# Deferring the first softmax map's normalisation to the merge, and putting each head's query and key projections next to each other

## The chip, the cores and the metric

The kernel runs on one core of a Trainium2 chip. The metric is the device time of one execution in microseconds, as the median of several executions. Before the change it is 1486.3 us (median of three, 1482.65 to 1487.47).

The core has five engines that run their own instruction lists in order and wait for each other through semaphores: PE (TensorE, matmuls, with its weight loads shown as PEld), DVE (VectorE), ACT (ScalarE), POOL (GpSimd) and SP (SyncE, which here only issues DMAs). PSUM holds what PE writes; SBUF holds everything else on chip.

## The reference

One layer of a streaming encoder works on 1024 new frames of a prompt and 32 frames of a running stream (together T = 1056 columns), with a model width of 1024. One wide input projection feeds two parallel branches, a gated linear attention (GLA, four heads) and a differential attention (eight heads); a merge joins them. In short, for the differential branch:

```python
s = einsum('bqhmd,bkhmd->bhmqk', q, k) * DIFF_HD ** -0.5     # m = 0, 1: two maps per head
p = softmax(where(mask, s, -inf), axis=-1)
attn = p[:, :, 0] - lam * p[:, :, 1]
o_diff = einsum('bhqk,bkhe->bqhe', attn, v)
yd = rmsnorm(o_diff, diff_subln_g) * (1 - lambda_init) * silu(dg)
merged = sigmoid(ma) * (yg @ w_proj_gla) + sigmoid(mb) * (yd @ w_proj_diff)
y = x + rmsnorm(merged @ w_out, post_norm_g)
```

`rmsnorm` divides by sqrt(mean square + EPS) over the 128 values of a head. The queries and keys are rotated (RoPE) over the first 16 of each map's 64 dimensions. The rotated keys and the values are outputs too.

## The kernel before

Every float32 matmul is done as three matmuls on a rounded high part and a remainder (`wh`, `wl` for weights; slots 0 and 1 of `X` for the input), so a 128-row block of a projection is 8 k-steps x 3 matmuls x 3 chunks of 352 columns.

The work has four stages. First the input is normalised and the value projections run (to about 240 us of the profiled execution). Then come the GLA heads (to about 557 us), the differential heads (to about 1180 us), and the merge: GLA output projection (`pg_first`, `pg_job`), differential output projection (`proj` with `BLK_PD`), and the output projection `wout`.

**The order on PE.** In the GLA and differential stages the order of PE's instructions is written out by a small planner, the class `Order` (`S`). Threads are generators; each `yield` gives a step's assumed cost, the events it needs with an assumed latency (table `W`), and the PSUM banks it takes. `S.run` always picks the first thread in its list that is ready in its own clock: the attention thread `diff_main`, then `sample_thread`, then `fill`. The plan is made when the program is built; on the chip PE follows the list in order and waits wherever an operand is late. The other engines' lists are laid out by the framework, with a higher priority for some copies.

**Jobs.** `fill` works through a list of projection jobs. For each chunk it takes one of two PSUM banks `pj`, issues 24 matmuls (L465 to L467) and calls the job's `evac`, which copies the bank; the planner has the bank back 1.5 us later (`w_pj`). A job's weights are loaded and split (L431 to L435) one job ahead. There are four sorts in the differential stage:

- `rot_job` for a query block (`split_q`) or key block (`split_k`): `evac` copies each chunk into the tile `rr` (L806, ACT). After the third chunk `done` copies four strips of `rr` into `sw` by DMA (L798, L799), multiplies `sw` on POOL (L800), does the rotation on DVE (L802, L804) and then splits `r` into high and low parts on ACT and DVE (L814 to L821 for the query, L833 to L841 for the key, the latter with a store of the key and four DMAs that copy the parts to the other half of the partitions). The tile `rr` has one buffer, so the next `rot_job`'s first copy follows the last reader of the one before. The query's parts have two buffers by head, the key's one.
- `dgate_job`: the silu gate of a head (L477, L478).
- `gate_job`: one block of the merge's sigmoid gates (L484), stored to memory at its end; the tile has one buffer.

The order of the jobs is the list built at L1037 to L1048: for each head the next head's query, one merge gate, the next head's key, this head's silu gate, and further merge gates where `GATES_DIFF` has more than one.

**Attention.** For each head and each block of 128 queries, `diff_scores` computes both maps' scores for w = 128 x (i + 1) keys (L883, L884), masks a corner (L885), takes the row maximum (L887), and exponentiates with the row sum accumulated (L889). Then one reciprocal of both sums (L892), one multiply of the second map (L893) and one multiply-add (L894) give the difference of the normalised maps. `diff_main` transposes it (L931), splits it (L933, L934) and multiplies by the values (L944 to L946). `diff_fin` takes the mean square of a head's output (`ps_m`, L859), stores it as a row of `msd`, multiplies the output by the silu gate and stores it to `ydd`.

**The merge's norm.** At L1130 to L1134 the eight rows of mean squares are loaded, turned into 1/sqrt(mean + EPS) by a logarithm and an exponential on ACT, stored to `rsd`, and read back broadcast over partitions (`rsb`, L1140); L1141 multiplies each head's `ydr` with it, then it is split into `Y` (L1069, L1070) for the differential output projection (L443 to L445).

Of the kernel before, what the change touches and what calls it, by code (L numbers as in the profile page):

```python
# [11 lines left out]
F32 = mybir.dt.float32  # L12
F32R = mybir.dt.float32r
I32 = mybir.dt.int32
AF = mybir.ActivationFunctionType
ALU = mybir.AluOpType
# [4 lines left out]
P = 128  # L21
NP = 1024
# [6 lines left out]
DH, HD = 8, 64  # L29
NQ = NP // P  # L30
EPS = 1e-6
# [20 lines left out]
W = {  # L52
# [3 lines left out]
    "tr_t": 2.27, "dv": 5.65, "at": 2.45, "pv_o": 1.1, "sdg": 1.84, "sdk": 21.35, "kc": 7.45, "ss_s": 3.69,  # L56
    "sp": 7.1, "st_t": 1.14, "sv": 3.44, "spt": 0.43, "so_o": 3.58, "so": 4.1, "so_t": 0.72, "yg0": 4.48,
    "yg": 1.18, "pg_b": 1.72, "sm": 1.98, "sm_w": 0.00141, "sm_s": 2.25, "p": 2.4, "p_w": 0.00204,
}


# [61 lines left out]
def hybrid_step_kernel(ctx: ExitStack, tc: tile.TileContext, a):  # L123
    nc = tc.nc
    mm = nc.tensor.matmul
    act = nc.scalar.activation
    ve = nc.vector
    dma = nc.sync.dma_start
    st = nc.sync.dma_start
# [4 lines left out]
    dram = ctx.enter_context(tc.tile_pool(name="dram", bufs=1, space=DRAM))  # L134
    cst = ctx.enter_context(tc.tile_pool(name="cst", bufs=1))
# [9 lines left out]
    def tbank(name):  # L145
        return pp.tile([P, 512], F32, tag="t", name=name)
# [5 lines left out]
    ident = cst.tile([P, P], F32, name="ident")  # L152
    make_identity(nc, ident)
    eps = cst.tile([P, 1], F32, name="eps")
# [23 lines left out]
    ptd = dram.tile([KT, P, T], F32, name="ptd")  # L178

    msd = dram.tile([DH, NP], F32, name="msd")  # L180
    rsd = dram.tile([DH, NP], F32, name="rsd")


# [7 lines left out]
    v1 = pool("v1")  # L191
# [138 lines left out]
    with tc.manual_schedule(engines={E.PE, E.Activation, E.DVE, E.Pool}):  # L330

        def warm(n):
            ps = obank("ps_warm")
            for _ in range(n):
                mm(ps[:, 0:P], one_h, one_h, start=True, stop=True)
        warm(10)
        norm_square(0)
        s = norm_scale(0)
        warm(9)
        w0 = value_weights(0)  # L340

        def weights(n):
            for _ in range(n):
                wv = next(w0)
            return wv
        weights(2)
        norm_apply(*s, 0)
        weights(1)
        norm_low(*s, 0)
        weights(2)  # L350
        norm_apply(*s, 1)
        norm_low(*s, 1)
        weights(3)
        norm_square(1)
        wv = weights(3)
        ps = bank("ps_v")

        def first(p, ks):
            for k in ks:
                mm(ps, xs[k][:, p == 1, 0:P], wv[p == 2][:, k, :], start=(p == k == 0), stop=(p == 2 and k == KT - 1))  # L360
        first(0, range(6))
        first(1, range(6))
        s = norm_scale(1)
        norm_apply(*s, 0)
        weights(1)
        norm_apply(*s, 1)
        for p, ks in ((0, (6, 7)), (1, (6, 7)), (2, range(8))):
            first(p, ks)
        norm_low(*s, 0)
        norm_low(*s, 1)  # L370
        norm_square(2)
        w0 = value_weights(1)
        nxt = weights(1)
        for i in range(1, NQ + 1):
            value_tile(0, i - 1, ps)
            if i == NQ:
                xsm = sample_pair(xs, "xsm")

            def meanwhile():
                norm_tile(i + 1)  # L380
                if i < NQ - 1:
                    norm_square(i + 2)
                if i in (3, 4, 5, 6):
                    weights(3 if i < 6 else 2)
            ps = value_mm(i, *wv, meanwhile)
        value_tile(0, NQ, ps)
        wgs = gate_weights()

        gg_half = cst.tile([P, 2], F32, name="gg_half")
        ve.tensor_scalar(gg_half, g_gla, 0.5, None, op0=ALU.mult)  # L390
        gs_half = cst.tile([P, 1], F32, name="gs_half")
        ve.tensor_scalar(gs_half, g_sub, 0.5 * (1.0 - LAM_INIT), None, op0=ALU.mult)


        lv = cst.tile([P, 4, HD], F32, name="lv")
        dma(lv, a["lamv"].unsqueeze(0).to_broadcast([P, 4, HD]))
        lp = cst.tile([P, 2, HD], F32, name="lp")
        ve.tensor_tensor(lp, lv[:, 0:2, :], lv[:, 2:4, :], op=ALU.mult)
        ls = cst.tile([P, 2], F32, name="ls")
        ve.tensor_reduce(ls, lp, axis=AX.X, op=ALU.add)  # L400
        le = cst.tile([P, 2], F32, name="le")
        act(le, ls, AF.Exp)
        neglam = cst.tile([P, 1], F32, name="neglam")
        ve.tensor_tensor(neglam, le[:, 1:2], le[:, 0:1], op=ALU.subtract)
        ve.tensor_scalar(neglam, neglam, LAM_INIT, None, op0=ALU.subtract)
        coef = cst.tile([P, 1], F32, name="coef")
        ve.memset(coef, 1.0)
        for r in (32, 96):
            ve.tensor_copy(coef[r : r + 32], neglam[r : r + 32])
        wv = nxt  # L410
# [9 lines left out]
    tp = pool("tp", side="right", reuse_waits="tile")  # L420


    S = Order({"pj": 2, "s": 2, "t": 1, "o": 1})
# [57 lines left out]
    def gate_job(b, w, j):  # L481
        def begin():
            th = rp.tile([P, T], F32, tag="gate", name="gate")
            return (lambda ps, sl: act(th[:, sl], ps, AF.Tanh, scale=0.5)), (lambda: st(thd[w, j], th))  # L484
        return b, ("gate", w, j), begin, []
# [242 lines left out]
    gates = [(BLK_MB + j, 1, j) for j in range(KT)] + [(BLK_MA + j, 0, j) for j in range(KT)]  # L728
# [18 lines left out]
    jobs = []  # L747
# [33 lines left out]
    def sam(n, h):  # L781
        return smp[:, 20 + 4 * n + h % 4, :]

    dqs, dks, dsg = {}, {}, {}

    def parts(n, cnt):
# [82 lines left out]
    def diff_scores(h, i, out):  # L869
        w = (i + 1) * P  # L870
        qsl = slice(i * P, i * P + P)
        qs, (ks, kls) = dqs[h], dks[h]
        sm = dp.tile([P, 2], F32, tag="sm", bufs=2, name="sm")
        pt = []
        soft = W["sm"] + w * W["sm_w"]
        for m in range(2):
            cost = sum(max(0.11, min(512, w - n0) / 2200) for n0 in range(0, w, 512)) * 2
            yield cost, [(("dk", h), W["dk"]), (("dq", h), W["dq"])], ["s"]
            ps = dbank("ps_s")

            for n0 in range(0, w, 512):
                n = min(512, w - n0)
                mm(ps[:, n0 : n0 + n], qs[m][:, qsl], ks[m][:, n0 : n0 + n], start=True, stop=False)  # L883
                mm(ps[:, n0 : n0 + n], qs[m][:, qsl], kls[m][:, n0 : n0 + n], start=False, stop=True)  # L884
            ve.memset(ps[0:64, w - 64 : w], -1e30)  # L885
            nm = dp.tile([P, 1], F32, tag=f"nm{m}", bufs=2, name="nm")
            ve.tensor_reduce(nm, ps[:, 0:w], axis=AX.X, op=ALU.max, negate=True)  # L887
            p = dp.tile([P, NP], F32, tag=f"p{m}", bufs=2 - m, name="p")
            act(p[:, 0:w], ps[:, 0:w], AF.Exp, bias=nm, accum_out=sm[:, m : m + 1])  # L889
            S.free("s", soft + W["sm_s"])  # L890
            pt.append(p)
        ve.reciprocal(sm, sm)  # L892
        ve.tensor_scalar(pt[1][:, 0:w], pt[1][:, 0:w], sm[:, 1:2], neglam, op0=ALU.mult, op1=ALU.mult)  # L893
        ve.scalar_tensor_tensor(pt[0][:, 0:w], pt[0][:, 0:w], sm[:, 0:1], pt[1][:, 0:w], op0=ALU.mult, op1=ALU.add)  # L894
        S.mark(("p", h, i))
        if i == NQ - 1:
            S.mark(("qk", h))
        out[i] = pt[0], soft + W["p"] + w * W["p_w"]

    def diff_main():  # L900
        fin = None
        for h in range(DH):
# [47 lines left out]
                S.mark(("pv", h, g))  # L950
            fin = diff_fin(h, osb, sqo)
        yield from fin

    def sample_thread():
        w = PAST + NS
# [82 lines left out]
    for h in range(-1, DH):  # L1038
        need = [(("qk", h - 1), 0.0)] if h >= 1 else []
        n = GATES_DIFF[h + 1]  # L1040
        if h + 1 < DH:
            jobs.append(rot_job(BLK_DQ + h + 1, ("dq", h + 1), need, split_q(h + 1)))
        jobs += [gate_job(*gates.pop(0)) for _ in range(min(n, 1))]
        if h + 1 < DH:
            jobs.append(rot_job(BLK_DK + h + 1, ("dk", h + 1), need, split_k(h + 1)))
        if h >= 0:
            jobs.append(dgate_job(h))
        jobs += [gate_job(*gates.pop(0)) for _ in range(n - 1)]  # L1048
    with tc.manual_schedule(engines=PE):
        left = S.run(left + [[diff_main(), None, first], [sample_thread(), None, nullcontext],  # L1050
                             [fill(jobs, xs), None, nullcontext]],
# [75 lines left out]
    Y = x_pair("Y")  # L1127
    yd = [Y[k // 6][:, k % 6] for k in range(KT)]

    rs = cp.tile([DH, NP], F32, tag="cwh", name="rs")  # L1130
    dma(rs, msd)
    act(rs, rs, AF.Ln, bias=eps[0:DH])
    act(rs, rs, AF.Exp, scale=-0.5)
    st(rsd, rs)  # L1134
    rsb = {}
# [165 lines left out]
```

## Time and profile before

| What | Value |
|---|---|
| Median of three runs | 1486.3 us (1482.65 to 1487.47) |
| The profiled execution's own time | 1483.59 us |
| Its span, first to last instruction | 1481.9 us |
| Mean granted TensorE clock | 0.99 |
| PE busy | 1422.6 us, 96% of the span |
| DVE busy | 786.6 us, 53% |
| ACT busy | 601.0 us, 41% |
| POOL busy | 298.4 us, 20% |

How to read the rows. A row of a stretch has the stretch, its length, then for PE, PEld, DVE, ACT and POOL the busy microseconds with the number of instructions, then the granted TensorE clock (1.00 is full speed), the DMA engines' busy share and the GB/s that they moved. A row of a group has the line, engine and operation, what is written from what, shapes and count; behind the bar the busy microseconds in all, the mean nanoseconds of one, and the idle time of the engine just before them with what ended it. A row of a timeline has start and duration in microseconds, engine, line and operation; the bracket is the idle time of the engine before it and what ended that. A wait for several semaphores is put down to one of them, so the name in a bracket can be another than the true one. PE's matmuls are pipelined and their durations overlap.

### The profile page before, as it was taken

Reading aid. Unit: us, or ns where it says so; the run is one execution under the profiler, and the core shown is the slowest. Engines: PE = TensorE matmul, PEld = TensorE weight load, DVE = VectorE, ACT = ScalarE, POOL = GpSimd, SP = SyncE. Lnnn points to the kernel's source line nnn. Section 1 sums busy time; section 2 is a strip of 40 time slices with the busy share of each in tenths; the row PEclk is TensorE's granted clock in tenths of the full one; section 3 lists DMA queues with packets and bytes.
Section 4 is the critical chain, followed back from the end, with each engine's and each line's share of the span. In section 5 each row is a group of like instructions: output and inputs, shape, how many; then the busy total and the mean of one; then the engine's idle time right before and its main releaser. Section 6 shows DMA issues by size and latency. Waiting matters only on the chain.

```text
span 1481.9 us, 22365 instructions
## 1 busy us (share of the span) xinstructions
PE 1422.6 (96%) x8848; PEld 1327.6 (90%) x8848; DVE 786.6 (53%) x1464; ACT 601.0 (41%) x1262; POOL 298.4 (20%) x186
## 2 busy tenths in 40 slices
PE   8999999989999999899999999999899899999997
PEld 6787789889989899899989998998899799999997
DVE  5702005755565343576767767678665535455415
ACT  5612114535344232455555555555455432221311
POOL 1200002222213224123222222222221111122001
PEclk9999999999999999999999999999999999999999
DMA  8621111122222233323232333223322278633205
GB/s 310 205 105 38 45 45 48 56 74 68 81 70 73 70 120 108 90 62 106 72 108 60 106 86 96 69 83 90 92 68 81 97 264 302 223 131 129 103 1 192
DMA packets 66742, 156.58 MB, mean 106 GB/s; under 512 B 10008, under 2 KB 28568, under 8 KB 65600
## 3 DMA queue, kind: packets, MB, share of 16 engines
q1 hardware_dynamic: 66624, 155.01, 32.3%
q8 instruction: 74, 1.21, 0.3%
q14 instruction: 44, 0.36, 0.1%
HBM read 104.39 MB, written 40.04 MB: 97 GB/s over the span
## 4 chain that ended last, share of the span: by engine, by line
PE 51%; DVE 6%; DMA 4%; ACT 2%; issue 1%; POOL 1%; SPq 0%; DVEq 0%; POOLq 0%; ACTq 0%
PE ps_w L465 9%; PE ps_w L466 9%; PE ps_w L467 9%; PE ps_w L444 2%; PE ps_w L443 2%; PE ps_w L445 2%; PE ps_s L884 2%; PE ps_t L931 2%; PE ps_s L883 2%; DMA ydr<-ydd 2%; PE ps_c L1193 2%; PE ps_c L1195 2%; PE ps_c L1194 2%; PE po L945 1%; PE po L946 1%
## 5 line engine op out<-in xcount | busy, mean ns | idle before, releaser
L465 PE MATMUL ps_w<-X,wh 128*128 128x352 f32 x1344 | 453.8, 338 | 8.5 <-DVE sg L478 3.2
L466 PE MATMUL ps_w<-X,wl 128*128 128x352 f32 x1344 | 438.2, 326 | 0.0
L467 PE MATMUL ps_w<-X,wh 128*128 128x352 f32 x1344 | 436.4, 325 | 0.0
L435 POOL TENSOR_TENSOR wl<-wr,wh 128x1024 fp32r<-128x1024 f32 x72 | 179.5, 2493 | 661.8 <-ACT wh L433 528.6
L465 PEld LDWEIGHTS ps_w<-X,wh 128*128 128x128 f32 x1344 | 255.8, 190 | 13.6 <-issue 4.9
L466 PEld LDWEIGHTS ps_w<-X,wl 128*128 128x128 f32 x1344 | 256.1, 191 | 1.2 <-issue 1.2
L467 PEld LDWEIGHTS ps_w<-X,wh 128*128 128x128 f32 x1344 | 255.1, 190 | 0.0
L889 ACT ACTIVATE p<-ps_s,nm 128x256 f32<-128x256 f32 (+7 forms) x128 | 94.6, 741 | 59.1 <-DVE ps_s L885 31.1
L286 PE MATMUL ps_v<-wh,X 128*128 128x512 f32 x248 | 97.6, 393 | 0.6 <-DVE X L225 0.6
L287 PE MATMUL ps_v<-wl,X 128*128 128x512 f32 x248 | 98.0, 395 | 0.0
L433 ACT ACTIVATE wh<-wr 128x1024 fp32r<-128x1024 f32 x72 | 75.9, 1054 | 54.6 <-PE ps_w L467 30.4
L285 PE MATMUL ps_v<-wh,X 128*128 128x512 f32 x248 | 97.9, 395 | 0.0
L887 DVE TENSOR_REDUCE nm<-ps_s 128x1 f32<-128x256 f32 (+7 forms) x128 | 94.8, 747 | 2.7
L272 DVE TENSOR_TENSOR vo<-ps_v,vo 32x512 f32<-32x512 f32 x4 | 2.7, 679 | 139.9 <-ACT vo L271 139.9
L885 DVE MEMSET ps_s<- 64x64 f32 x128 | 14.3, 112 | 115.8 <-PE ps_s L884 114.2
L650 POOL TENSOR_TENSOR vl<-vr,vh 128x512 fp32r<-128x512 f32 (+1 forms) x20 | 24.8, 1242 | 222.8 <-DVE t L516 160.3
L883 PE MATMUL ps_s<-k,q 128*128 128x512 f32 (+2 forms) x192 | 68.0, 362 | 1.2 <-DMA k<-k 1.2
L884 PE MATMUL ps_s<-kl,q 128*128 128x512 f32 (+2 forms) x192 | 63.8, 348 | 3.9 <-DMA kl<-kl 3.4
L268 ACT ACTIVATE vo<-ps_v 128x512 f32<-128x512 f32 x32 | 19.1, 596 | 114.2 <-PE ps_v L287 113.8
L933 ACT ACTIVATE ah<-ps_t 128x512 fp32r<-128x512 f32 (+2 forms) x96 | 46.9, 488 | 43.6 <-PE ps_t L931 43.0
L934 DVE TENSOR_TENSOR al<-ps_t,ah 128x512 fp32r<-128x512 f32 (+2 forms) x96 | 53.1, 554 | 18.6 <-ACT ah L933 17.3
L444 PE MATMUL ps_w<-Y,wl 128*128 128x352 f32 x192 | 62.2, 324 | 0.0
(319 smaller groups left out, 2960.9 us busy)
## 6 DMA issues: line engine op xcount, KB each, us to landing
wr<-w SPq DMA_DIRECT2D x72, 512.0 KB
thd<-gate SPq DMA_DIRECT2D x16, 528.0 KB
xn<-xn SPq DMA_DIRECT2D x16, 512.0 KB
wr<-wv SPq DMA_DIRECT2D x16, 512.0 KB
newk<-rr SPq DMA_DIRECT2D x8, 528.0 KB
ygr<-ygd SPq DMA_DIRECT2D x8, 528.0 KB
tha<-thd SPq DMA_DIRECT2D x8, 528.0 KB
ydr<-ydd SPq DMA_DIRECT2D x8, 528.0 KB
```

Of the source, the lines that this page charges most:

```text
L285: mm(ps, xk[:, 0, t0 : t0 + P], wh[:, k, :], start=(k == 0), stop=False)
L286: mm(ps, xk[:, 1, t0 : t0 + P], wh[:, k, :], start=False, stop=False)
L287: mm(ps, xk[:, 0, t0 : t0 + P], wl[:, k, :], start=False, stop=(k == KT - 1))
L435: nc.gpsimd.tensor_tensor(wl, wr, wh.bitcast(F32), op=ALU.subtract)
L444: mm(ps[:, :n], wl[:, k, :], src[k][:, 0, t0 : t0 + n], start=False, stop=False)
L465: mm(ps[:, :n], wh[:, k, :], src[k][:, 0, t0 : t0 + n], start=(k == 0), stop=False)
L466: mm(ps[:, :n], wl[:, k, :], src[k][:, 0, t0 : t0 + n], start=False, stop=False)
L467: mm(ps[:, :n], wh[:, k, :], src[k][:, 1, t0 : t0 + n], start=False, stop=(k == KT - 1))
L883: mm(ps[:, n0 : n0 + n], qs[m][:, qsl], ks[m][:, n0 : n0 + n], start=True, stop=False)
L884: mm(ps[:, n0 : n0 + n], qs[m][:, qsl], kls[m][:, n0 : n0 + n], start=False, stop=True)
L887: ve.tensor_reduce(nm, ps[:, 0:w], axis=AX.X, op=ALU.max, negate=True)
L889: act(p[:, 0:w], ps[:, 0:w], AF.Exp, bias=nm, accum_out=sm[:, m : m + 1])
```

## The change

Three things change.

The softmax of a block no longer divides the first map by its row sum. The first map's sum s0 goes into a column of a new tile `s0a` (one column per head and block). The second map is scaled by neglam x s0 / s1, computed in two one-column operations, and one multiply-add gives the difference, which is then larger by the factor s0 than before in each row. The wide multiply L893 is gone.

The factor is taken out in the merge's norm. The norm of a row scaled by s0 is the same if EPS is scaled by s0 squared. After the last head `s0a` is transposed on PE, copied, and stored to a new memory tensor `s0d`; in the merge it is loaded beside `msd`, EPS x s0 squared is formed and added on DVE, and the logarithm has no bias any more.

The jobs' order for each head becomes: the next head's query, the next head's key, this head's silu gate, then all of its merge gates. Beside that, the planner's assumed latency of a block (`p`, `p_w`) gets new numbers, and two small constants' tiles (`lv`, `lp`) use rotating buffers of the first stage.

```diff
-    ... "sm_s": 2.25, "p": 2.4, "p_w": 0.00204,
+    ... "sm_s": 2.25, "p": 2.2, "p_w": 0.00145,
...
+    s0d = dram.tile([DH, NP], F32, name="s0d")
...
-        lv = cst.tile([P, 4, HD], F32, name="lv")
+        lv = v1.tile([P, 4, HD], F32, tag="xn", bufs=2, name="lv")
...
-        lp = cst.tile([P, 2, HD], F32, name="lp")
+        lp = v1.tile([P, 2, HD], F32, tag="xr", bufs=2, name="lp")
...
+    s0a = tp.tile([P, DH * NQ], F32, name="s0a")
+    s0t = tp.tile([DH * NQ, P], F32, name="s0t")
...
-        sm = dp.tile([P, 2], F32, tag="sm", bufs=2, name="sm")
+        sm = dp.tile([P, 1], F32, tag="sm", bufs=2, name="sm")
+        s0 = s0a[:, h * NQ + i : h * NQ + i + 1]
...
-            act(p[:, 0:w], ps[:, 0:w], AF.Exp, bias=nm, accum_out=sm[:, m : m + 1])
+            act(p[:, 0:w], ps[:, 0:w], AF.Exp, bias=nm, accum_out=sm if m else s0)
...
         ve.reciprocal(sm, sm)
-        ve.tensor_scalar(pt[1][:, 0:w], pt[1][:, 0:w], sm[:, 1:2], neglam, op0=ALU.mult, op1=ALU.mult)
-        ve.scalar_tensor_tensor(pt[0][:, 0:w], pt[0][:, 0:w], sm[:, 0:1], pt[1][:, 0:w], op0=ALU.mult, op1=ALU.add)
+
+        ve.scalar_tensor_tensor(sm, sm, neglam, s0, op0=ALU.mult, op1=ALU.mult)
+        ve.scalar_tensor_tensor(pt[0][:, 0:w], pt[1][:, 0:w], sm, pt[0][:, 0:w], op0=ALU.mult, op1=ALU.add)
...
         yield from fin
+        yield 0.11, [], ["t"]
+        ps = tbank("ps_s0")
+        nc.tensor.transpose(ps[0 : DH * NQ, 0:P], s0a, ident)
+        act(s0t, ps[0 : DH * NQ, 0:P], AF.Copy)
+        S.free("t", W["tr_t"])
+        st(s0d.rearrange("h (i q) -> (h i) q", q=P), s0t)
...
             jobs.append(rot_job(BLK_DQ + h + 1, ("dq", h + 1), need, split_q(h + 1)))
-        jobs += [gate_job(*gates.pop(0)) for _ in range(min(n, 1))]
-        if h + 1 < DH:
             jobs.append(rot_job(BLK_DK + h + 1, ("dk", h + 1), need, split_k(h + 1)))
         if h >= 0:
             jobs.append(dgate_job(h))
-        jobs += [gate_job(*gates.pop(0)) for _ in range(n - 1)]
+        jobs += [gate_job(*gates.pop(0)) for _ in range(n)]
...
-    rs = cp.tile([DH, NP], F32, tag="cwh", name="rs")
+    rs2 = cp.tile([DH, 2, NP], F32, tag="cwh", name="rs")
+    rs, s0 = rs2[:, 0], rs2[:, 1]
     dma(rs, msd)
-    act(rs, rs, AF.Ln, bias=eps[0:DH])
+    dma(s0, s0d)
+    ve.scalar_tensor_tensor(s0, s0, EPS, s0, op0=ALU.mult, op1=ALU.mult)
+    ve.tensor_tensor(rs, rs, s0, op=ALU.add)
+    act(rs, rs, AF.Ln)
     act(rs, rs, AF.Exp, scale=-0.5)
     st(rsd, rs)
```

More of the change, by code (lines that the diff above doesn't have):

```diff
@@ L57 @@
     "sp": 7.1, "st_t": 1.14, "sv": 3.44, "spt": 0.43, "so_o": 3.58, "so": 4.1, "so_t": 0.72, "yg0": 4.48,
-    "yg": 1.18, "pg_b": 1.72, "sm": 1.98, "sm_w": 0.00141, "sm_s": 2.25, "p": 2.4, "p_w": 0.00204,
+    "yg": 1.18, "pg_b": 1.72, "sm": 1.98, "sm_w": 0.00141, "sm_s": 2.25, "p": 2.2, "p_w": 0.00145,
 }
```

## The prediction

> **What bounds the kernel now.** I read the page's busy times first, then the busy times by stretch through the differential-attention stage (560 to 1200 us), then that stage's groups by line, then the timelines of single engines around one head's query projection.
>
> ```profile
> PE 1422.6 (96%) x8848; PEld 1327.6 (90%) x8848; DVE 786.6 (53%) x1464; ACT 601.0 (41%) x1262; POOL 298.4 (20%) x186
> ...
> 560.00:760.00 200.00, 194.94 (x1237) 187.50 (x1236) 122.00 (x243) 98.53 (x220) 55.70 (x24) 0.98 0.32 93
> 760.00:960.00 200.00, 196.43 (x1259) 185.90 (x1259) 144.82 (x281) 107.80 (x247) 49.15 (x24) 1.00 0.27 80
> 960.00:1160.00 200.00, 193.31 (x1243) 182.39 (x1242) 134.59 (x265) 100.72 (x235) 47.72 (x22) 0.99 0.27 81
> 1160.00:1200.00 40.00, 35.15 (x213) 30.77 (x212) 19.74 (x29) 19.41 (x34) 3.56 (x4) 0.96 0.57 188
> ```
>
> TensorE bounds it. In the four stretches (length, then busy PE, PEld, DVE, ACT, POOL, then granted clock) PE is idle for 5.06 + 3.57 + 6.69 + 4.85 = 20.2 us, and the clock column takes at most another 0.02 x 200 + 0.01 x 200 + 0.04 x 40 = 7.6 us. So **27.8 us is the ceiling of what any reordering or relief of another engine can win here**; DVE, at most 72% busy, bounds no stretch. A loss has no such ceiling: PE runs one list in order, and every wait put into it is added to the span.
>
> **Part 1, the order of the jobs.** Query and key projection of a head share one tile, `rr`, with one buffer. The key job's first output copy (L806) must wait until the rotation and `split_q` have read all of the query job's `rr`. Before, a gate job lies between the two. Here is head 0's query job and what follows it:
>
> ```profile
> 560.53 0.46 ACT L806 ACTIVATE rr<-ps_w 128x352 f32<-128x352 f32 x1 [5.04 <-PE ps_w L467]
> 561.06 0.82 SPq L798 DMA_DIRECT2D sw<-rr  x1
> 563.77 0.62 SPq L799 DMA_DIRECT2D sw<-rr  x1
> 566.35 2.48 POOL L800 TENSOR_TENSOR sw<-sw,stb 128x1056 f32<-128x1056 f32 x1 [1.95 <-DMA sw<-rr]
> 570.01 1.38 DVE L804 TENSOR_TENSOR rr<-rr,sw 128x352 f32<-128x352 f32 x3
> 572.45 0.62 ACT L814 ACTIVATE q<-rr 64x512 fp32r<-64x512 f32 x1
> 575.26 0.69 DVE L818 SCALAR_TENSOR_TENSOR q<-rr,q 64x512 fp32r<-64x512 f32 x1
> ...
> 564.38 0.47 ACT L484 ACTIVATE gate<-ps_w 128x352 f32<-128x352 f32 x1 [2.43 <-PE ps_w L467]
> 568.25 0.47 ACT L484 ACTIVATE gate<-ps_w 128x352 f32<-128x352 f32 x1 [3.40 <-PE ps_w L467]
> 568.05 0.33 PE L465 MATMUL ps_w<-X,wh 128*128 128x352 f32 x1
> ```
>
> The last query chunk is copied by 560.99; then four small DMAs, the product on POOL, three sums on DVE, eight split operations: `rr` is read to the end at 575.95, a chain of 15.0 us. A chunk of a job takes PE 568.25 - 564.38 = 3.87 us, there are two `pj` banks, so the third chunk of the job behind the query needs the first one's bank back; the gate job began its third chunk at 568.05. The planner gives a bank back 1.5 us after the chunk (`w_pj`) and knows nothing of `rr`, so it will place the key job's matmuls exactly there. That the wait is real shows where `rr` is late already:
>
> ```profile
> 1028.29 0.42 DVE L836 TENSOR_TENSOR kl<-rr,k 64x256 fp32r<-64x256 f32 x1
> 1028.88 0.47 ACT L806 ACTIVATE rr<-ps_w 128x352 f32<-128x352 f32 x1 [3.69 <-PE ps_t L931]
> ```
>
> ACT stood 3.69 us in front of a query job's first copy and went 0.17 us after DVE's last read of the old `rr` (1028.71). *Head 0:* free at 575.95, less the 1.06 us that ACT came late (L804 ended 571.39, L814 began 572.45 behind a gate copy), plus 0.17, plus the copy's 0.47: 575.5. PE wants the bank at 568.05 and has no attention work yet: **+7.5 us** (8.5 if ACT is as late as now).
>
> *Heads 1 to 7.* Attention is interleaved, so both sides stretch. The chain of the first and the last of the seven, with the third chunk of the job that follows, which I read from the key jobs (the planner costs all jobs alike and attention starts one job earlier relative to the list, so the key job meets about the attention work that it meets now):
>
> ```profile
> 614.95 0.47 ACT L806 ACTIVATE rr<-ps_w 128x352 f32<-128x352 f32 x1 [1.37 <-PE ps_w L467]
> 633.64 1.12 DVE L818 SCALAR_TENSOR_TENSOR q<-rr,q 64x512 fp32r<-64x512 f32 x1
> 629.39 0.47 ACT L484 ACTIVATE gate<-ps_w 128x352 f32<-128x352 f32 x1
> 641.97 0.41 PE L465 MATMUL ps_w<-X,wh 128*128 128x352 f32 x1
> ...
> 1046.43 0.46 ACT L806 ACTIVATE rr<-ps_w 128x352 f32<-128x352 f32 x1 [0.42 <-PE ps_w L467]
> 1067.09 0.69 DVE L818 SCALAR_TENSOR_TENSOR q<-rr,q 64x512 fp32r<-64x512 f32 x1
> 1066.01 0.45 ACT L484 ACTIVATE gate<-ps_w 128x352 f32<-128x352 f32 x1
> 1079.76 0.41 PE L465 MATMUL ps_w<-X,wh 128*128 128x352 f32 x1
> ```
>
> Chains: 634.76 - 615.42 = 19.3 and 1067.78 - 1046.89 = 20.9, mean 20.1. From the previous job's last copy to the third chunk: 641.97 - 629.86 = 12.1 and 1079.76 - 1066.46 = 13.3, mean 12.7. Stall with the chain as it is: 20.1 + 0.6 - 12.7 = 8.0; with the undisturbed 15.0: 2.9. While PE stands, attention's operations on DVE and ACT run dry and the chain quickens, so I take the middle rounded down, 5: 7 x 5 = **+35 us** (bounds 20 and 56). Behind PE's waiting matmul everything is queued, attention's too; behind ACT's waiting copy are the exponentials, which then lack nothing that PE could use.
>
> *The clock.* Idle time costs twice:
>
> ```profile
> 499.06 0.40 PE L465 MATMUL ps_w<-X,wh 128*128 128x352 f32 x1 [2.06 <-PEq L579]
> 497.00:507.00 10.00, 7.94 (x43) 7.89 (x42) 4.61 (x7) 3.08 (x6) 1.77 (x1) 0.83 0.27 83
> ...
> 440.30 0.43 PE L465 MATMUL ps_w<-X,wh 128*128 128x352 f32 x1 [1.91 <-DVE sg L478]
> 436.00:446.00 10.00, 8.09 (x49) 7.19 (x48) 6.25 (x16) 4.04 (x6) 1.07 (x2) 1.00 0.27 87
> ```
>
> A gap of 2.06 us lowered the granted clock to 0.83 over ten us, 1.7 us of work; a gap of 1.91 us did not. Eight stalls of 5 us and more: 8 x 1.7 = **+13.6 us** (bounds 1.7, head 0 alone, and 13.6). The Trainium skill (TensorE: Matmul & The Clock Gate, Part 1, the HAM clock gate) would have the clock halved only after a whole idle window of about 3.4 us and calls gaps up to about 3 us safe. By it, stalls at my lower bound of 2.9 us would cost no clock and the sum would be 11.9 us lower; the gap of 2.06 us above disagrees with it, and the row decides.
>
> *What the order gives back.* A query job now comes two jobs, not one, behind the key job whose split holds `rr`, so waits like the 3.69 us go; keys are ready earlier; and attention runs one job ahead, which leaves projections to fill the end, where the last 40 us hold 4.85 us of idle. Of the 27.8 us ceiling I take a third: **-9 us** (bounds 0 and -27.8).
>
> **Part 2, the softmax.**
>
> ```profile
> L893 DVE TENSOR_SCALAR p<-p,sm,neglam 128x128 f32<-128x128 f32 (+3 forms) x64 | 43.0, 673 | 1.8
> L892 DVE RECIPROCAL sm<-sm 128x2 f32<-128x2 f32 x64 | 10.4, 163 | 18.1 <-ACT p L889 17.2
> L999 DVE TENSOR_TENSOR r<-r,coef 128x1 f32<-128x1 f32 x4 | 1.0, 238 | 0.1
> ```
>
> 64 wide operations go, 43.0 us of DVE; 64 one-column ones come, priced by L999 at 0.24 us: 15.2 us. The reciprocal and the wide sum stay. DVE is freed by 28 us that lie beside a busier PE: 0 on the path, its shorter latency being part of the third above. The planner's new weights shorten a block's assumed latency by 0.2 + 0.00059 w, 0.5 us at w = 512, against 0.67 - 0.24 = 0.43 us really saved: no cost. Moving `lv` and `lp` into rotating buffers, one transpose and one small store: under 1 us together, beside PE's list, 0.
>
> **Part 3, the merge's norm.**
>
> ```profile
> 1212.85 1.06 ACT L1133 ACTIVATE rs<-rs 8x1024 f32<-8x1024 f32 x1
> 1219.70 0.38 SPq L1140 DMA_DIRECT2D rsb<-rsd  x1
> 1268.83 1.25 DVE L1070 TENSOR_TENSOR Y<-ydr,Y 128x1056 fp32r<-128x1056 f32 x1
> 1285.72 0.33 PE L443 MATMUL ps_w<-Y,wh 128*128 128x352 f32 x1
> ```
>
> A load beside `msd` and two DVE operations on 8x1024 (about L1070's 1.25 us each) lengthen the chain to `Y` by some 3 us; `Y` is done at 1270.1, PE wants it near 1285.7. Covered by the gla output projection: 0. Without that cover 3; and if the new DVE operations wait for their load in front of the copies of that projection, at most the 6 us between issue and use of such a load, less one chunk's 3.87: bounds 0 and +3.
>
> **The sum.** Profiled execution 1483.6 (span 1481.9): 1483.6 + 7.5 + 35 + 13.6 - 9 = 1530.7, so **1531 us**. The median of the runs shown, 1486.3, lies 2.7 above the profiled one, well inside my bounds. Its own range is 1503 (7.5 + 20 + 1.7 - 9 makes 1504) to 1556 (8.5 + 56 + 13.6 - 5).
>
> **Rivals.**
> *Faster: attention fills the gap.* If the planner puts enough attention between the query job's end and the key job's third chunk (from 15.6 us on, against 12.7 now), the seven stalls vanish and half of the ceiling is won: 1483.6 + 7.5 + 1.7 - 14 = 1479. For it: in heavy blocks chunks come 6 us apart. Against: the spacing was below 13.4 in both rows.
> *Keys late as well.* Head 0 shows that the planner's 14.3 us (`W["dk"]`) is short:
>
> ```profile
> 583.69 0.47 ACT L806 ACTIVATE rr<-ps_w 128x352 f32<-128x352 f32 x1 [3.40 <-PE ps_w L467]
> 602.76 0.45 PE L884 MATMUL ps_s<-kl,q 128*128 128x128 f32 x1 [2.20 <-DMA kl<-kl]
> ```
>
> Keys took 602.76 - 584.16 = 18.6 us. If attention, a little faster, catches up with the keys, each of seven heads waits 4.3 us more: 1531 + 30 = 1561, up to 1580 with the clock.
> *It cancels.* Small stalls, about 2 us, and as much won: 1484. The change not doing what it says would end here too.
>
> **How the numbers follow.** Forecast 0.62, late keys 0.14, faster 0.16, cancels 0.08. A difference under 0.3% (4.5 us) can't be told from none: faster 0.16, same 0.08, slower 0.76. The range leaves out the faster rival and the tail of the late keys: 1482 to 1570.
>
> **What would show it.** Right: PE idle in front of L465 in the third chunk of each key job, released by ACT's `rr` copy, 3 to 8 us, eight times; PEclk at 9 or less in those slices; PE's busy time nearly unchanged, the span longer; L893 gone and no shorter span for it. Wrong: key copies that start within a us of their chunk's last matmul; or idle mostly in front of L883 and L884 on `kl` (late keys); or new idle behind 1200 us.

## The result and the profile after

After the change the kernel takes 1557.9 us (median of four runs, 1555.75 to 1560.02) against 1485.8 us before in the same comparison (1482.65 to 1487.47). The ratio is 1.0488, with a 95% interval of 1.0464 to 1.0511: the change makes the kernel 72 us slower. The profiled execution takes 1557.2 us with a span of 1555.4 us, 73.5 us more than the span before. The forecast was 1531; the range of 1482 to 1570 holds the result, the forecast's own range ends 2 us short of it.

In the new kernel the lines are shifted: L465 is L466, L806 is L809, L804 is L807, L818 is L821, L883 and L884 are L887 and L888, L931 is L936, L1009 is L1020. L893 is gone, L898 is the new one-column operation and L899 the multiply-add (L894 before).

First the page's busy times and the four stretches of the new kernel, in the columns of the rows shown before:

```profile
PE 1444.9 (93%) x8849; PEld 1347.6 (87%) x8849; DVE 757.9 (49%) x1466; ACT 599.7 (39%) x1263; POOL 300.8 (19%) x186
...
560.00:760.00 200.00, 176.37 (x1069) 169.94 (x1070) 106.23 (x221) 86.75 (x194) 47.24 (x21) 0.92 0.26 76
760.00:960.00 200.00, 186.16 (x1165) 177.00 (x1163) 123.07 (x262) 99.80 (x231) 45.11 (x21) 0.97 0.27 79
960.00:1160.00 200.00, 175.39 (x1074) 164.72 (x1075) 108.55 (x235) 89.22 (x205) 43.44 (x19) 0.92 0.24 69
```

PE is idle for 23.6, 13.8 and 24.6 us in three stretches that had 5.1, 3.6 and 6.7, and the clock is 0.92 to 0.97 where it was 0.98 to 1.00. These stretches no longer hold the same work, so for the account I cut both kernels at the same events: the end of the GLA attention, the first matmul of the GLA output projection, the first of the differential output projection, the end. The new kernel:

```profile
562.20:1258.70 696.50, 631.56 (x3893) 597.19 (x3891) 384.84 (x812) 322.08 (x732) 153.14 (x71) 0.94 0.27 80
1258.70:1359.40 100.70, 94.54 (x577) 92.44 (x577) 46.52 (x51) 26.38 (x27) 21.45 (x8) 1.00 0.73 254
1359.40:1555.40 196.00, 188.28 (x1410) 187.83 (x1408) 86.45 (x161) 44.51 (x119) 24.21 (x24) 0.99 0.35 117
```

The kernel before, cut at the same events:

```profile
557.60:1183.50 625.90, 607.29 (x3887) 576.12 (x3886) 412.48 (x809) 318.09 (x726) 156.12 (x72) 0.99 0.29 87
1183.50:1285.70 102.20, 98.19 (x580) 94.23 (x581) 47.80 (x52) 31.36 (x32) 16.98 (x7) 0.98 0.76 266
1285.70:1481.90 196.20, 188.27 (x1410) 187.82 (x1408) 86.63 (x161) 44.50 (x119) 24.21 (x24) 0.99 0.34 117
```

The differential stage is **70.6 us** longer (696.5 against 625.9). Of these, 46.3 are idle time of PE (64.9 against 18.6, length less busy) and 24.3 are busy time: the same matmuls, run longer at the lower clock. The rest of the span's 73.5 us is a later start of the stage, 4.6 us, and a gain of 1.7 us behind it. The later start I do not count to the change: of the kernels below, one that has the change's whole text ahead of this stage began it at 557.4, and one that has the old text there at 561.0.

PE's waits in that stage (line, what was waited for, us in total, times, longest), first of the new kernel:

```profile
PE ps_w L466 <- ACT rr L809: 48.3, 8, 9.5
PE ps_s L888 <- DMA kl<-kl: 7.7, 6, 2.2
PE ps_t L936 <- DVE smp L1020: 5.1, 1, 5.1
```

and of the kernel before:

```profile
PE ps_t L931 <- DVE al L934: 4.1, 3, 1.4
PE ps_st L1006 <- DVE smp L1009: 3.6, 2, 2.3
PE ps_s L884 <- DMA kl<-kl: 3.4, 3, 2.2
```

The wait for `rr` was not there at all; now it comes eight times and is 48.3 of 64.9 us. The others add up to 16.6 us, hardly less than the 18.6 of before: keys (`kl`) are waited for longer than before, and a single wait of 5.1 us in front of an attention transpose is new (the first experiment shows where it comes from).

The timeline of the new kernel at the key jobs of head 0, head 1 and head 7:

```profile
565.19 0.47 ACT L809 ACTIVATE rr<-ps_w 128x352 f32<-128x352 f32 x1 [5.05 <-PE ps_w L468]
574.86 2.52 POOL L918 TENSOR_TENSOR vl<-vr,vh 128x1024 fp32r<-128x1024 f32 x1 [0.92 <-ACT vh L917]
575.11 3.53 DVE L807 TENSOR_TENSOR rr<-rr,sw 128x352 f32<-128x352 f32 x3
582.41 0.66 PE L466 MATMUL ps_w<-X,wh 128*128 128x352 f32 x1 [9.54 <-ACT rr L809]
...
634.31 0.46 ACT L809 ACTIVATE rr<-ps_w 128x352 f32<-128x352 f32 x1 [2.59 <-PE ps_w L468]
650.91 0.69 DVE L821 SCALAR_TENSOR_TENSOR q<-rr,q 64x512 fp32r<-64x512 f32 x1
651.68 0.82 ACT L809 ACTIVATE rr<-ps_w 128x352 f32<-128x352 f32 x2 [1.84 <-issue]
652.20 0.66 PE L466 MATMUL ps_w<-X,wh 128*128 128x352 f32 x1 [5.03 <-ACT rr L809]
651.59:658.42 6.83, 6.22 (x20) 5.74 (x21) 2.20 (x5) 1.04 (x3) 0.00 (x0) 0.50 0.00 0
...
1134.85 0.66 PE L466 MATMUL ps_w<-X,wh 128*128 128x352 f32 x1 [6.51 <-ACT rr L809]
```

Read head 1 from top to bottom. The query's last chunk is copied by 634.77. DVE makes its last read of that `rr` until 651.60. ACT's copy of the key's first chunk goes at 651.68, 0.08 us later, and PE's matmul, which needs the bank, 0.52 us behind it, after 5.03 us of nothing. The matmul takes 0.66 us where such a one took 0.33 at full clock, and from 651.59 on, for 6.83 us, the clock is granted at one half (the row of that stretch; PE is busy for 6.22 us of it). ACT's own wait is labelled with "issue" and says nothing; that its copy starts 0.08 us after DVE's last read of the old tile is what names the cause.

### The profile page after: what moved, and what is told of

Read it like the earlier page. It is cut to its first block, busy times and chain, and to the rows that moved or that the text cites. A ratio compares the mean times of both kernels' runs of the same rounds, so it can differ in the third digit from the quotient of the medians.

```text
span 1555.4 us, 22380 instructions
## 1 busy us (share of the span) xinstructions
PE 1444.9 (93%) x8849; PEld 1347.6 (87%) x8849; DVE 757.9 (49%) x1466; ACT 599.7 (39%) x1263; POOL 300.8 (19%) x186
## 4 chain that ended last, share of the span: by engine, by line
PE 48%; DVE 8%; DMA 5%; ACT 3%; issue 2%; POOL 1%; SPq 0%; DVEq 0%; POOLq 0%; ACTq 0%
PE ps_w L466 9%; PE ps_w L467 8%; PE ps_w L468 8%; PE ps_s L888 2%; PE ps_s L887 2%; PE ps_w L445 2%; PE ps_w L444 2%; PE ps_w L446 2%; PE ps_t L936 2%; DMA ydr<-ydd 2%; DMA kl<-kl 1%; PE ps_c L1206 1%; PE ps_c L1208 1%; PE ps_c L1207 1%; PE ps_m L862 1%
## 5 line engine op out<-in xcount | busy, mean ns | idle before, releaser
L466 PE MATMUL ps_w<-X,wh 128*128 128x352 f32 x1344 | 463.1, 345 | 56.8 <-ACT rr L809 48.3
L467 PE MATMUL ps_w<-X,wl 128*128 128x352 f32 x1344 | 444.0, 330 | 0.0
L468 PE MATMUL ps_w<-X,wh 128*128 128x352 f32 x1344 | 441.7, 329 | 0.0
L466 PEld LDWEIGHTS ps_w<-X,wh 128*128 128x128 f32 x1344 | 260.9, 194 | 66.0 <-ACT rr L809 50.5
L467 PEld LDWEIGHTS ps_w<-X,wl 128*128 128x128 f32 x1344 | 261.4, 194 | 2.1 <-issue 2.0
L468 PEld LDWEIGHTS ps_w<-X,wh 128*128 128x128 f32 x1344 | 260.0, 193 | 0.0
L893 ACT ACTIVATE p<-ps_s,nm 128x256 f32<-128x256 f32 (+7 forms) x128 | 94.6, 742 | 35.1 <-DVE nm L891 18.8
L888 PE MATMUL ps_s<-kl,q 128*128 128x512 f32 (+2 forms) x192 | 66.5, 361 | 8.2 <-DMA kl<-kl 7.7
L887 PE MATMUL ps_s<-k,q 128*128 128x512 f32 (+2 forms) x192 | 70.1, 372 | 3.3 <-DMA k<-k 1.7
```

The source lines that it names most:

```text
L466: mm(ps[:, :n], wh[:, k, :], src[k][:, 0, t0 : t0 + n], start=(k == 0), stop=False)
L467: mm(ps[:, :n], wl[:, k, :], src[k][:, 0, t0 : t0 + n], start=False, stop=False)
L468: mm(ps[:, :n], wh[:, k, :], src[k][:, 1, t0 : t0 + n], start=False, stop=(k == KT - 1))
L893: act(p[:, 0:w], ps[:, 0:w], AF.Exp, bias=nm, accum_out=sm if m else s0)
```

## The experiments

All kernels here compute the whole layer. Each ratio is to the kernel before, run on the same chip at the same time. "Old weights" are the planner's numbers `p` 2.4 and `p_w` 0.00204 of before, "new weights" the change's 2.2 and 0.00145. The theory is that the new order's wait for `rr` makes the loss; the rivals put it into the softmax and the planner, or into late keys.

**The change without its order.**

```diff
+        jobs += [gate_job(*gates.pop(0)) for _ in range(min(n, 1))]
+        if h + 1 < DH:
             jobs.append(rot_job(BLK_DK + h + 1, ("dk", h + 1), need, split_k(h + 1)))
...
-        jobs += [gate_job(*gates.pop(0)) for _ in range(n)]
+        jobs += [gate_job(*gates.pop(0)) for _ in range(n - 1)]
```

> The changed kernel with the jobs' order of before (query, gate, key, silu gate), softmax and norm as changed. Theory (the one rr buffer between adjacent query and key): the eight waits of PE for the rr copy, 48.3 us, and the 24.6 us of half clock behind them go, so 1558 - 73 = 1485 us, between 1476 and 1488, with no PE wait on the rr copy over 1 us. Rival (the deferred sum: one-column DVE operations and the shorter planned latencies make attention late): the loss stays, 1530 us or more.

Measured: 1499.7 us, ratio 1.0094 (1.0066 to 1.0121). Most of the loss goes with the order and the waits for `rr` are gone, but 14 us stay, where I had expected none. Its stage and its longest waits there:

```profile
564.20:1200.70 636.50, 610.53 (x3869) 580.17 (x3867) 384.96 (x805) 315.41 (x721) 151.21 (x70) 0.98 0.29 85
...
PE ps_s L888 <- DMA kl<-kl: 9.0, 8, 2.2
PE ps_t L936 <- DVE smp L1020: 5.0, 1, 5.0
PE ps_so L1040 <- DVE os__8566 L1036: 3.8, 1, 3.8
```

The stage is 10.6 us longer than before, and it waits for keys. Something in Part 2, whose cost I had put at 0, costs this. The two single waits come from the order of DVE's work:

```profile
962.07 0.42 DVE L1020 TENSOR_TENSOR smp<-ps_st,smp 128x256 f32<-128x256 f32 x1
962.64 1.03 PE L936 MATMUL ps_t<-ident,p 128*128 128x128 f32 x4 [5.04 <-DVE smp L1020]
...
782.44 0.27 DVE L1036 TENSOR_SCALAR os__8566<-os__8566,ss 64x128 f32<-64x128 f32 x1
782.86 0.33 PE L1040 MATMUL ps_so<-ident,os__8566 64*128 64x64 f32 x1 [3.82 <-DVE os__8566 L1036]
```

The transposes of the running stream (`ps_st`) and of attention (`ps_t`) share one PSUM bank. DVE reads it for the running stream (L1020) only behind the eight operations of a key split that began at 958.46, and PE's next transposes stand until then. The other wait is for L1036, which stands in DVE's list behind a multiply-add of 2.87 us; that one is slowed beside POOL (last section).

**The order alone, in the kernel before.**

```diff
-        jobs += [gate_job(*gates.pop(0)) for _ in range(min(n, 1))]
-        if h + 1 < DH:
             jobs.append(rot_job(BLK_DK + h + 1, ("dk", h + 1), need, split_k(h + 1)))
...
-        jobs += [gate_job(*gates.pop(0)) for _ in range(n - 1)]
+        jobs += [gate_job(*gates.pop(0)) for _ in range(n)]
```

> The kernel before with nothing changed but the jobs' order. Theory: it loses what the whole change lost, 1486 + 71 = 1557 us, between 1545 and 1565, with eight PE waits on the rr copy of 5 to 10 us each. Rival (the deferred sum): at most 1495 us.

Measured: 1541.9 us, ratio 1.0389 (1.0352 to 1.0426). The order makes 58 of the 72 us by itself. That is less than the whole and 3 us under the expected range, as the run above had shown from its side.

```profile
561.00:1247.70 686.70, 623.43 (x3881) 590.73 (x3879) 405.39 (x807) 319.52 (x724) 153.45 (x70) 0.95 0.27 79
...
PE ps_w L465 <- ACT rr L806: 52.5, 8, 9.3
```

**The key job in a buffer of its own.** The key job takes the gates' tile instead of `rr`; order, softmax and weights are those of the change.

```diff
-            r = dp.tile([P, T], F32, tag="rr", name="rr")
+            if event[0] == "dk":
+                r = rp.tile([P, T], F32, tag="gate", name="rk")
+            else:
+                r = dp.tile([P, T], F32, tag="rr", name="rr")
```

> The changed kernel, order as changed, but the key job copies into the tile of the merge gates instead of rr, so that query and key have a buffer each. Theory: PE's waits on that copy fall from 48.3 us to under 8, most of the half clock goes with them, 1485 to 1500 us. Rival (it is the order as such: keys and attention fall out of step with the plan, and waits for the key's copies or the scores take the place): 1520 us or more, with the idle time in front of the scores (L887 and L888 of the changed kernel).

Measured: 1490.7 us, ratio 1.0046 (1.0031 to 1.0061). This is the cleanest evidence for the mechanism: the jobs stay neighbours, PE's matmuls write the same tiles in the same order in both traces, only the shared tile is gone, and 67 us come back. What is left of that kind is one wait, head 0's, where a merge gate that now shares its tile with the key follows the key directly:

```profile
PE ps_w L466 <- ACT gate L485: 9.0, 1, 9.0
```

**Another job between the two.** Query, silu gate, key, merge gates.

```diff
-            jobs.append(rot_job(BLK_DK + h + 1, ("dk", h + 1), need, split_k(h + 1)))
+            pass
         if h >= 0:
             jobs.append(dgate_job(h))
+        elif n:
+            jobs.append(gate_job(*gates.pop(0)))
+            n -= 1
+        if h + 1 < DH:
+            jobs.append(rot_job(BLK_DK + h + 1, ("dk", h + 1), need, split_k(h + 1)))
```

> The changed kernel with a head's silu gate between its next query and key, all merge gates behind the key. Theory (any job of three chunks between the two covers the chain of 15 to 20 us): like the old order within 8 us, 1478 to 1495 us. Rival (it must be a merge gate, whose copy is one ACT operation, and the silu gate's DVE operations make the chain late): 1510 us or more with PE waits on the rr copy.

Measured: 1498.1 us, ratio 1.0086 (1.0061 to 1.0111), within 2 us of the kernel with the old order and 3 us above the expected range. No wait for `rr` is left. So a silu gate between the two does it as a merge gate does, for heads 1 to 7; head 0 has no silu gate before it and gets a merge gate here too.

**Half of the pairs apart.** For heads 0 to 3 a merge gate stands between query and key, for heads 4 to 7 they are adjacent.

```diff
             jobs.append(rot_job(BLK_DQ + h + 1, ("dq", h + 1), need, split_q(h + 1)))
+            if h + 1 < 4:
+                jobs += [gate_job(*gates.pop(0)) for _ in range(min(n, 1))]
+                n -= 1
```

> The changed kernel with a gate job between query and key for heads 0 to 3 and the two adjacent for heads 4 to 7 only. Theory (each adjacent pair costs its own wait for rr and the half clock behind it, independent of the others): four waits of 5 to 6.5 us, 24 us together, and some 3 us each for the clock, above the 1499.7 us of the changed kernel with the old order: 1535 us, between 1525 and 1543. Rival (the loss starts at head 0 and grows from attention falling out of step): under 1515 us.

Measured: 1511.1 us, ratio 1.018 (1.0158 to 1.0201), 24 us less than expected and where the rival had put the time. But its mechanism is not what the trace shows, for the four waits are there:

```profile
PE ps_w L466 <- ACT rr L809: 20.9, 4, 5.6
PE ps_s L888 <- DMA kl<-kl: 2.7, 2, 2.2
```

but the key waits of the kernel with the old order (9.0 us) have fallen to 2.7, and its 5.0 us in front of a transpose are gone (the 3.8 us for L1036 are not). So the 14 us of the first run are no fixed price that adds to the order's.

**The old weights in the old order.** Of the change only the sum, the merge's norm and the constants' tiles are left.

```diff
-    "p": 2.2, "p_w": 0.00145,
+    "p": 2.4, "p_w": 0.00204,
```

(with the old order's lines as above)

> The changed kernel with the old order and also the planner's old latency of a block (2.4 + 0.00204 w); only the deferred sum and the norm are left of the change. Theory (the shortened latencies bring attention to the next head before its keys are there): back to 1485 us, within 5. Rival (the deferred sum itself costs, through the order of the DVE list): 1495 to 1502 us as with the new latencies.

Measured: 1486.6 us, ratio 1.0001 (0.9983 to 1.0019).

```profile
561.40:1183.80 622.40, 605.83 (x3888) 575.14 (x3886) 389.30 (x809) 317.88 (x726) 152.49 (x72) 0.99 0.30 87
...
PE ps_s L888 <- DMA kl<-kl: 2.7, 2, 2.2
```

Two numbers in a table of the planner are the whole difference to the first run: 14.1 us of the stage, of which 4.7 are busy time at a lower clock. PE's matmuls write the same tiles in the same order as in the kernel before, but for the one added transpose, so this run also prices the deferred sum by itself: it is free within the interval of 0.2%, and wins nothing either, although DVE does 23.2 us less in the stage than before.

**Keys that the planner expects later.** The first run's kernel with its new weights, and `W["dk"]` at 20 instead of 14.32.

```diff
-    "dk": 14.32,
+    "dk": 20.0,
```

> The changed kernel with the old order, and 20.0 instead of 14.32 us as the planner's latency from a key job's end to its scores. Theory (PE's waits for the key's copies, 12 us of them in front of the scores, and the half clock behind the three longest make up the loss of 14 us that the old order leaves): these waits fall under 3 us, 1482 to 1488 us. Rival (attention starts later and the end of the stage is late instead): 1495 us or more.

Measured: 1491.9 us, ratio 1.0045 (1.0025 to 1.0064), between what the theory and what the rival had said. The waits for `kl` are down to 0.2 us, and about half of the 14 us is back. The other half is not. A wait for L1036 of 3.8 us is there as in the first run, only at a later head, and a wait of the GLA output projection's first matmul, behind the attention, for its operand's split on ACT has grown from 1.4 us:

```profile
PE ps_w L1110 <- ACT y L1080: 7.9, 1, 7.9
```

**The order and the sum, with the old weights.** The change as it is, with the one line of weights above.

> The whole change but for the planner's latency of a block, which is the old one (2.4 + 0.00204 w). Theory (order and latencies cost separately, 57 and 13 us): 1558 - 13 = 1545 us, between 1538 and 1550. Rival (PE's waits for rr give attention the time that the short latencies take from it, so that these cost nothing beside the waits): 1553 us or more.

Measured: 1533.1 us, ratio 1.0357 (1.0323 to 1.0391); times 1485 this is 1538, the lower end of the expected range.

```profile
557.40:1235.70 678.30, 622.19 (x3882) 590.03 (x3880) 383.69 (x807) 318.64 (x725) 149.93 (x70) 0.95 0.27 80
...
PE ps_w L466 <- ACT rr L809: 46.2, 8, 9.1
PE ps_s L888 <- DMA kl<-kl: 3.6, 3, 2.1
```

The new weights cost 18.2 us of the stage here (696.5 less 678.3). Beside the kernel with the order alone, whose matmuls come in the same order but for one transpose, the waits for `rr` are 6.3 us shorter (46.2 against 52.5); that DVE's relief shortens the chain would fit, but the intervals of the two ratios overlap.

**Half of the pairs apart, old weights.** The edit of the half-adjacent kernel with the line of weights.

> Deferred sum, old latencies, query and key adjacent for heads 4 to 7 only. Theory: four waits for rr of 5 to 5.6 us, 21 us, and about 3 us each of half clock behind them, above the 1486.6 us of the same kernel without an adjacent pair: 1519 us, between 1512 and 1524, which is half of what eight cost. Rival (waits hide others, as with the short latencies, where four cost 11 us): 1495 to 1505 us.

Measured: 1518.2 us, ratio 1.0237 (1.0214 to 1.0261), inside the expected range. Against the kernel with old order and old weights (1.0001), four adjacent pairs cost 0.0236 x 1485 = 35 us, 8.8 each, of which 6.7 are the wait itself:

```profile
PE ps_w L466 <- ACT rr L809: 26.8, 4, 6.7
```

Note the sign: in this order the old weights are the slower ones (1.0237 against 1.018).

**Only head 0's pair adjacent, old weights.**

```diff
+            if h + 1 > 0:
+                jobs += [gate_job(*gates.pop(0)) for _ in range(min(n, 1))]
+                n -= 1
```

> Deferred sum, old latencies, query and key adjacent for head 0 only, where no attention work lies beside. Theory: one wait of 9.5 us, of which the half clock behind it costs another 2 us: 1486.6 + 11.5 = 1498 us, between 1494 and 1501. Rival (head 0's keys are early by one job, attention and all after it start earlier, and the end gets the time back): 1490 us or less.

Measured: 1532.4 us, ratio 1.0332 (1.0308 to 1.0356), far above what was expected. The one wait for `rr` has the size expected; the rest is new:

```profile
563.90:1230.00 666.10, 614.52 (x3866) 582.12 (x3864) 381.40 (x806) 316.57 (x721) 158.26 (x71) 0.97 0.27 82
...
PE ps_s L888 <- DMA kl<-kl: 16.2, 15, 2.9
PE ps_w L466 <- ACT rr L809: 9.1, 1, 9.1
PE ps_w L1111 <- ACT y L1081: 8.5, 1, 8.5
PE ps_s L887 <- DMA k<-k: 3.8, 2, 2.5
```

With head 0's key moved ahead by a job, attention can start a job earlier, while the other heads' keys keep their places in the list. Keys are then waited for 20 us in all (16.2 and 3.8, in 17 waits), and 8.5 us go at the stage's end. That the earlier start is the cause is an argument from the list of jobs; the run shows only the waits.

**Own buffer, and a gate between for head 0.** The buffer of its own for the keys of heads 1 to 7, and head 0's key in `rr` behind a merge gate; first with the new weights.

```diff
+            if event[0] == "dk" and event[1]:
+                r = rp.tile([P, T], F32, tag="gate", name="rk")
...
+            if h < 0:
+                jobs.append(gate_job(*gates.pop(0)))
+                n -= 1
```

> The changed kernel, key jobs of heads 1 to 7 in the tile of the merge gates, and for head 0, whose key is followed by a merge gate at once, a gate between query and key as before. Theory: the single 9.0 us wait that was left (the gate job behind head 0's key waiting for the shared tile) and its half clock go: 1490.7 - 9.0 - 3 = 1479 us, between 1474 and 1484. Rival (the wait moves to head 0's keys or elsewhere): 1488 us or more.

Measured: 1486.7 us, ratio 1.0017 (1.0005 to 1.0029), 3 us above the expected range. All of the loss but 0.2% is repaired; nothing is won. With the old weights:

> Deferred sum, old latencies, order as changed with the key job of heads 1 to 7 in the tile of the merge gates and a gate between head 0's query and key. With a buffer for each the order costs nothing: theory 1480 to 1488 us; it beats the kernel before only if the two waits of 2.3 us in the sample's transposes and 4.7 us for the shared tile shrink too. Rival (the old latencies are too long for this order): 1490 us or more.

Measured: 1514.4 us, ratio 1.0224 (1.0201 to 1.0247), as the rival had it. The plan that comes out places the merge gates so that they wait for the tile that they now share with the keys, seven times:

```profile
PE ps_w L466 <- ACT gate L485: 21.2, 7, 3.7
```

No kernel here is faster than the one before.

## Why the prediction was right, and where it fell short

**The order.** The mechanism, its place and its count are as predicted: eight waits of PE in front of L466 (L465 before), released by ACT's copy to `rr`, each as the old `rr` comes free. *Heads 1 to 7* cost 48.3 - 9.5 = 38.8 us, predicted 35; from 5.0 us at head 1 to 6.5 at head 7. Head 1's two sides are those of the working: the chain took 651.60 - 634.77 = 16.8 us (predicted between 15.0 and 20.1), and PE wanted the bank at 647.17, 12.4 us behind the query's last copy (predicted 12.7). So attention did not fill the gap, and the *faster* rival falls. *Head 0* cost 9.5 us, predicted 7.5: the three sums L807 took 3.53 us instead of 1.38, beside a product of POOL, 2.15 us that the working did not have.

**The clock** cost 24.3 us, predicted 13.6. I took the loss from a gap of 2.06 us, 1.7 us each. Behind the eight waits for `rr` PE is busy for 35.6 us at half clock, which loses half of it, 17.8 us or 2.2 each; so this term was somewhat too small. The rest of the clock's cost does not lie behind these waits. In four more stretches, behind three waits for keys and the 5.1 us wait in front of a transpose, PE is busy for 22.8 us at half clock and loses 11.4, where the kernel before lost 4.6 in two such stretches. One of the four, in the columns of the stretches:

```profile
986.10:992.93 6.83, 4.67 (x17) 4.70 (x18) 2.58 (x6) 1.10 (x3) 0.00 (x0) 0.50 0.67 170
```

With the old weights the term came to 14.9 us (622.19 less 607.29), so the rest comes with the next point.

**The planner's new weights** are the step that failed. Part 2 set 0.5 us assumed against 0.43 saved and concluded "no cost". The comparison was with the duration of an operation, but what the number sets is where in PE's list each attention step goes; there the two numbers were worth 14 us in the old order (1.0001 to 1.0094) and 18 us of the stage in the new one. With the old weights, the terms of the sum stand almost as written:

| Term | predicted | order and sum, old weights | the change |
|---|---|---|---|
| waits for `rr` | 42.5 | 46.2 | 48.3 |
| clock (busy time of PE) | 13.6 | 14.9 | 24.3 |
| what the order gives back (other idle time) | -9 | -8.7 | -2.0 |
| the stage | 47.1 | 52.4 | 70.6 |

The middle column is from the stage's rows: 678.30 - 622.19 = 56.1 idle, less 46.2, is 9.9 against 18.6 before. So other waits did shrink by 8.7 us beside the order (which of the three ways of the working did it is not shown), and the weights took most of that away again, with a lower clock beside it. Of the 26 us between the forecast and the profiled execution the weights make about 18, the later start of the stage 4.6, and the terms are 5.3 too small (52.4 against 47.1), less the 1.7 won behind the stage.

What the weights do is shown in part. In the old order the new waits are for keys (`kl` from 2.7 to 9.0 us) and the two single ones for DVE, 5.0 and 3.8 us; giving the planner later keys took the first away, and half of the loss. So the *late keys* rival, which I priced at 30 us, is real, but it is set off by the weights rather than by the order, and in the change it is 4.3 us (3.4 to 7.7) and some 6 us of the clock behind it. It came nearest to its size, 20 of 30 us, in the kernel with only head 0's pair adjacent. But the weights are not dear in themselves: with half of the pairs apart and with the keys' own buffer the new ones were faster, by 0.6% and 2.1%. How the 14 us divide among these waits, and which weights suit which order, stays open.

That the result lies inside the range of 1482 to 1570 is in part luck. The upper end was set for late keys behind the order, and what filled it was the planner's weights. The forecast's own range also takes -5 for what the order gives back, where the bounds of that term say 0; with 0 it would end at 1562 and hold the result.

**The softmax and the norm.** L893 is gone and no gain came of it, as predicted. Two groups of the new kernel's stage:

```profile
L899 DVE SCALAR_TENSOR_TENSOR p<-p,sm 128x128 f32<-128x128 f32 (+3 forms) x64 | 52.3, 817 | 2.0
L898 DVE SCALAR_TENSOR_TENSOR sm<-sm,neglam,s0a 128x1 f32<-128x1 f32 x64 | 19.4, 303 | 2.0
```

The one-column operation takes 0.303 us on average (taken as 0.24 from the nearest row); its median is 0.219, and six that fell beside POOL make the difference (last section). DVE does 27.6 us less in the stage (412.48 to 384.84; predicted 28). The merge's norm cost nothing: the two stretches behind the stage took 100.7 and 196.0 us against 102.2 and 196.2. The sum, the norm and the small constants together are the kernel with the old order and the old weights, ratio 1.0001. In Part 3 the time between issue and use of a load, 6 us in the working, is 6.6 in the trace of before (1219.70 to 1226.28), which changes nothing there.

**What would show it** held, with two exceptions. Head 0's wait of 9.5 us lies above the 3 to 8 us of the sign. And PE's busy time is not nearly unchanged but 22.3 us up (1422.6 to 1444.9), because a matmul at half the clock is counted as busy for twice as long. I had put the clock into the sum but not into this sign.

## What to carry to other kernels

When two producers that share a one-buffer tile become neighbours in an in-order list, set the last reader of the first against the moment when the engine wants its first PSUM bank back; the difference is the stall, and here the slower clock behind it added some 2.2 us to each. The wait shows on the engine that fills PSUM, and not with the tile's readers, so it is found by comparing the end of the last read with the start of the next copy. A planner's constant is an input to the order and not a duration: when one is changed, time that change alone, in the order in which it will be used.

## What the runs showed of the hardware

**The clock.** Behind the wait of 5.03 us the clock was granted at one half for 6.83 us. Each such stretch of the stage, in all traces of this case, lasts 3.41, 6.83 or 10.24 us, one to three times the same length: 10.24 behind head 0's 9.5 us, 3.41 behind head 5's 5.3, and 6.83 behind the other six. So the length does not simply follow the wait. The gap of 2.06 us in the trace of before cost 1.7 us, that is 3.41 us at half clock. The Trainium skill (TensorE: Matmul & The Clock Gate, Part 1, the HAM clock gate) gives an idle window of about 3.4 us as the condition and at least one busy window of about 3.4 us as the way back. The lengths measured here agree with such a window. The condition does not: the gap of 2.06 us lies below it, and in the kernel with half of the pairs apart a gap of 1.85 us (from 500.60) was followed by 3.41 us at half clock, while the gap of 1.91 us in the trace of before was not.

**DVE beside POOL.** In several places a DVE operation with two tiles as inputs, begun while POOL worked, stood until POOL was done. At head 0 POOL's product ran from 574.86 to 577.38; DVE's three sums, begun at 575.11, ended at 578.64, which is 1.26 us after POOL, close to the 1.38 that they take alone. Another case, of the change without its order, first the two instructions, then the groups of that form and of a wider one over the whole run:

```profile
779.23 2.61 POOL L436 TENSOR_TENSOR wl<-wr,wh 128x1024 fp32r<-128x1024 f32 x1 [4.70 <-ACT wh L434]
779.65 2.87 DVE L899 SCALAR_TENSOR_TENSOR p<-p,sm 128x640 f32<-128x640 f32 x1
...
L899 DVE SCALAR_TENSOR_TENSOR p<-p,sm 128x640 f32<-128x640 f32 x8 | 13.4, 1679 | 0.3
L899 DVE SCALAR_TENSOR_TENSOR p<-p,sm 128x768 f32<-128x768 f32 x8 | 8.2, 1019 | 0.3
```

POOL ends at 781.84 and DVE 0.68 us later; the narrower form takes 1.68 us on average and the wider 1.02. In the new kernel six of the 64 one-column operations took 0.52 to 1.72 us, and each ended within 0.02 us of the end of a POOL product. The Trainium skill (SBUF — State Buffer, section SBUF: two separate sides) calls the pair of ports that the two engines share an exclusive lock for the length of an instruction, and these rows agree with it. Here it was worth 2 us on the path at head 0, and in the case above it lengthened PE's wait of 3.8 us for L1036, the next operation of DVE's list. The other cases were not followed to PE.
